# Two heads' keys from one matmul product, and a weight load split in two

## The chip, the cores and the metric

The kernel runs on one core of a Trainium2 chip. The metric is the device time of one execution in microseconds (us), the median of several runs. The engines are named as in the profile: PE is TensorE (PEld its weight loads), DVE is VectorE, ACT is ScalarE, POOL is GpSimd, and SP is SyncE, which here issues DMAs.

## What is computed

Two layers of a bidirectional encoder over 512 tokens of width 1024. Each layer projects x once and runs three kinds of attention side by side; then one output projection, a layer norm, a feed-forward part and another layer norm. The change is in the first kind, multi-head latent attention with six heads:

```python
ckv = rms_norm(h[..., o0:o0 + MLA_KV_RANK], mla_kv_norm[l])          # 128 wide
kva = (ckv @ mla_w_ukv[l]).reshape(B, S, MLA_HEADS, MLA_NOPE_DIM + MLA_V_DIM)
k_rope = jnp.broadcast_to(rope(k_rope, pos), (B, S, MLA_HEADS, MLA_ROPE_DIM))
ka = jnp.concatenate([kva[..., :MLA_NOPE_DIM], k_rope], axis=-1)     # 64 + 32
va = kva[..., MLA_NOPE_DIM:]                                         # 64
out_a = dense_attention(qa, ka, va, (MLA_NOPE_DIM + MLA_ROPE_DIM) ** -0.5)
```

The weight `mla_w_ukv` has 768 columns: for each of the six heads 64 columns that make its keys and then 64 that make its values.

## The kernel before, in words

All products are done in a split form: an operand is held as a high part `hi` and a low remainder `lo`, and `mm3` (line 160) makes a product of three matmuls, hi x hi, hi x lo and lo x hi, into one PSUM bank. So every tile that goes into a product is first copied by ScalarE (the high part) and then subtracted on VectorE or GpSimd (the low part).

`wload` (line 140) loads a weight: one DMA on SP's queue into a raw tile, a copy on ScalarE into `whi`, a subtraction into `wlo`.

The attention of all 16 heads is run by `attend` (line 322): units of one head and 128 queries each follow each other. A unit has three steps that run some units apart: `a` makes the scores (`sc`, line 251), the row minimum on VectorE (`nm`, line 261), the exponential on ScalarE (`pl`, line 263) and the scaling on GpSimd (line 266); `b` transposes the weights on TensorE (`ptr`, line 274) and splits them (`PTh` on ScalarE, `PTl` on VectorE, line 282); `c` multiplies them with the values (`po`, lines 292 and 293). Between the units fillers are run, generators that do the projections and prepare later heads; the table `W` says from which unit to which. The framework's scheduler then sets the instructions of each engine in an order of its own, so a change in one place can move rows elsewhere.

Latent heads come last, units 40 to 63. What prepares them are fillers:

- `latent_qv` (line 588) loads the query weights and `w_ukv` (line 591), makes the queries (`uq`), and then, for each of four token tiles, the values of all heads (`uv`, line 609) from the value columns, which it picks out of the 768 by stride; `mv` (lines 375, 376) are the split values.
- `mla_T(h)` (line 537), once for each head, in two steps: it transposes the head's queries (`tT` into `qkT`), and then makes the head's keys: three matmuls with the 64 key columns of this head, 512 tokens wide, into a bank of `ps_mm`; a DMA puts the shared rotary part `krT` below (line 544), and ScalarE and VectorE split the 64 rows (lines 546, 547) into the tile `kT`:

```python
wk = [w[:, 0, h * P:h * P + HD] for w in wkv[0]]
r = pqk.tile([P, 2, T], F32R, tag="q", name="kT")
mm3(pb[:HD], wk, (latT[2][:, 0], latT[2][:, 1]), True, True)
```

Two pools set limits here: `ps_mm` has two PSUM banks, which `uq`, `uv`, `tT`, `kT` and the output projection's first part (`opp`, line 633) share in turn; `pqk` has four buffers for `qkT` and `kT`, also in turn.

Of the kernel before, what the change touches and what calls it, by code (L numbers as in the profile page):

```python
# [10 lines left out]
F32 = mybir.dt.float32  # L11
F32R = mybir.dt.float32r
AF = mybir.ActivationFunctionType
ALU = mybir.AluOpType
AX = mybir.AxisListType

P = 128
T = 512
# [6 lines left out]
HD = 64  # L25
# [54 lines left out]
def encoder(ctx: ExitStack, tc, x, w_in, mla_q_norm, mla_kv_norm, w_uq, w_ukv, gqa_q_norm, gqa_k_norm, rel_bias,  # L80
            w_out, ln1_g, ln1_b, w_gate, w_up, w_down, ln2_g, ln2_b, tabs, onehot, neglnc, out):
    nc = tc.nc
    V, A, G, TE = nc.vector, nc.scalar, nc.gpsimd, nc.tensor
    LO = {k: V if c == 'v' else G for k, c in LOE.items()}
# [10 lines left out]
    pqk = pool("pqk", 4)  # L95
# [10 lines left out]
    ps_mm = pool("ps_mm", 2, space=PS)  # L106
# [4 lines left out]
    def bank(pl, name):  # L111
        return pl.tile([P, 512], F32, tag="b", name=name)
# [24 lines left out]
             "m": ((pmix, "m"), (pmix, "m"))}  # L137
    turn = {"raw": 0}

    def wload(src, shape, lo, ring="w", raw="w"):  # L140

        n = shape[1] * shape[2]
        if raw == "wd":
            turn["raw"] += 1
            raw = "wwdd"[turn["raw"] % 4]
        (hp, ht), (lp, lt) = parts[ring]
        r = raws[raw][0].tile([P, 1024], F32, tag=raws[raw][1], name="wraw")
        nc.sync.dma_start(r[:, :n].rearrange("p (a c) -> p a c", a=shape[1]), src)
        h = hp.tile([P, 1024], F32R, tag=ht, name="whi")
        A.copy(h[:, :n], r[:, :n])  # L150
        o = lp.tile([P, 1024], F32R, tag=lt, name="wlo")
        step = n // 2 if lo is G and SPLIT else n
        for c in range(0, n, step):
            lo.tensor_tensor(o[:, c:c + step], r[:, c:c + step], h[:, c:c + step].bitcast(F32), op=ALU.subtract)  # L154
        return (h[:, :n].rearrange("p (a c) -> p a c", a=shape[1]), o[:, :n].rearrange("p (a c) -> p a c", a=shape[1]))

    def krows(w, k0, nk, c0, c1):
        return w[k0 * P:(k0 + nk) * P, c0:c1].rearrange("(k p) c -> p k c", p=P)

    def mm3(ps, a, b, first, last, more=False):  # L160

        ah, al = a
        bh, bl = b
        TE.matmul(ps, ah, bh, start=first, stop=False, skip_group_check=more)  # L164
        TE.matmul(ps, ah, bl, start=False, stop=False, skip_group_check=more)  # L165
        TE.matmul(ps, al, bh, start=False, stop=last, skip_group_check=more)  # L166
# [238 lines left out]
    for l in range(DEPTH):  # L405
# [131 lines left out]
        def mla_T(h):  # L537
            assert ("q", h // 3) in told
            to_T(lambda t: tq[h // 3][:, t, h % 3, :], 96, mqk[h])
            yield  # L540
            pb = bank(ps_mm, "kT")
            wk = [w[:, 0, h * P:h * P + HD] for w in wkv[0]]
            r = pqk.tile([P, 2, T], F32R, tag="q", name="kT")
            nc.sync.dma_start(r[HD:96].bitcast(F32), krT[0][:32].bitcast(F32))
            mm3(pb[:HD], wk, (latT[2][:, 0], latT[2][:, 1]), True, True)
            A.copy(r[:HD, 0], pb[:HD])
            V.tensor_tensor(r[:HD, 1], pb[:HD], r[:HD, 0].bitcast(F32), op=ALU.subtract)
            mqk[h].append(r)
            yield

        def dil_qk(pair):
# [36 lines left out]
        def latent_qv():  # L588
            tq.extend(pxt.tile([P, NT, 3, 96], F32, tag="x", name="tq") for _ in range(2))
            wq = [wload(krows(w_uq[l], 0, 2, 288 * c, 288 * c + 288), (P, 2, 288), LO['uq']) for c in range(2)]  # L590
            wkv.append(wload(krows(w_ukv[l], 0, 1, 0, 768), (P, 1, 768), LO['kv']))
            yield
            for c in range(2):
                h, o = wq[c]
                for t in range(NT):
                    pb = bank(ps_mm, "uq")[:, :288]
                    ts = slice(t * P, (t + 1) * P)
                    for k in range(2):
                        mm3(pb, (latT[k][:, 0, ts], latT[k][:, 1, ts]), (h[:, k], o[:, k]), k == 0, k == 1)
                    A.copy(tq[c][:, t], pb.rearrange("p (h c) -> p h c", h=3))  # L600
                    yield
                tm = ppl.tile([P, T], F32, tag="l", name="qrt")[:, :384].rearrange("p (t h c) -> p t h c", t=NT, h=3)
                rope32(tq[c][:, :, :, 64:96], 3, tm)
                told.append(("q", c))
            h, o = (w[:, 0].rearrange("p (h c) -> p h c", h=6)[:, :, HD:] for w in wkv[0])
            for t in range(NT):
                pb = bank(ps_mm, "uv")[:, :6 * HD]
                ts = slice(t * P, (t + 1) * P)
                mm3(pb, (latT[2][:, 0, ts], latT[2][:, 1, ts]), (h, o), True, True)
                vt = pv_sb.tile([P, 6, 2, HD], F32R, tag="v", name="mv")  # L610
                split_v(vt, pb.rearrange("p (a c) -> p a c", a=6))
                mv_.append(vt)
                yield
# [53 lines left out]


        latT, krT, tq, mv_, wkv, dts, told = [], [], [], [], [], {}, []
        gqk, dqk, mqk = ([[] for _ in range(n)] for n in (2, 3, 6))  # L670
        heads = []
        for h in range(6):
# [33 lines left out]
        lqv, op = latent_qv(), out_part()  # L706
# [312 lines left out]
```

## Time and profile before

| | |
|---|---|
| median of 3 runs | 1259.31 us (1258.02 to 1260.97) |
| the profiled execution's own time | 1259.3 us |
| its span in the profile | 1257.5 us |
| TensorE busy | 1222.3 us, 97% |
| VectorE busy | 871.6 us, 69% |
| ScalarE busy | 661.9 us, 53% |
| GpSimd busy | 491.9 us, 39% |
| data moved by DMA | 153.26 MB, mean 122 GB/s |

The span is what the profile's rows cover; the execution's time has 1.8 us around it. Layer 1 begins in the trace at some 640 us; the latent heads are prepared and run at 130 to 260 us and again at 745 to 895 us. A share of busy time is a mean over stages; a row of the chain of waits says what was on the path that ended last in a stretch, and a row of the timeline when an instruction started and how long its engine had waited before it. A matmul's recorded length overlaps the next one's, so the time that one takes from TensorE is read from start to start, or from the chain.

### The profile page before, as it was taken

The page shows a single profiled execution, that of the slowest core. Times are in us where ns is not written, and L with a number is a line of the kernel's source. Part 1 is how long each engine was busy: PE and PEld are TensorE (multiplying, and loading weights), DVE is VectorE, ACT ScalarE, POOL GpSimd, SP SyncE. Part 2 cuts the span into 40 slices and gives each one's busy share as a digit, 9 for nine tenths or more (in the row PEclk, how much of TensorE's full clock was granted, in tenths as well). Part 3 has the DMA queues.
Part 4 walks back from the last instruction along what each step waited for, and adds up shares of the span by engine and source line. Part 5 has one row for each costly group of instructions (what it writes and reads, how often), then busy time and mean ns, then how long its engine had stood idle before and what let it go on. Part 6 is the DMA issues. An engine that isn't in the chain of part 4 may idle for free.

```text
span 1257.5 us, 20806 instructions
## 1 busy us (share of the span) xinstructions
PE 1222.3 (97%) x7816; PEld 1108.8 (88%) x7816; DVE 871.6 (69%) x1512; ACT 661.9 (53%) x1273; POOL 491.9 (39%) x508
## 2 busy tenths in 40 slices
PE   8999899999999999999999998999999999999996
PEld 7789788889999889998888897888899988999985
DVE  4369998597875447773664889966987743677546
ACT  4366786553654235652445667855355632466422
POOL 0345575568442024300345466645574400341004
PEclk9899999999999999999999999999999999999998
DMA  6623310326988348834535231105199953685343
GB/s 184 172 81 93 89 35 13 106 84 137 191 185 193 107 102 177 163 87 129 179 96 145 85 105 40 37 12 159 57 182 183 192 164 92 127 184 126 107 153 117
DMA packets 167692, 153.26 MB, mean 122 GB/s; under 512 B 9340, under 2 KB 136444, under 8 KB 167592
## 3 DMA queue, kind: packets, MB, share of 16 engines
q1 hardware_dynamic: 121228, 111.98, 30.4%
q0 software_dynamic: 46208, 39.86, 18.1%
q8 instruction: 62, 1.02, 0.3%
q14 instruction: 38, 0.31, 0.1%
q10 hardware_dynamic: 156, 0.09, 0.0%
HBM read 145.06 MB, written 2.12 MB: 117 GB/s over the span
## 4 chain that ended last, share of the span: by engine, by line
PE 82%; DVE 7%; POOL 3%; ACT 3%; DMA 2%; issue 2%; SPq 1%; DVEq 0%; ACTq 0%; POOLq 0%
PE u L164 10%; PE u L165 10%; PE u L166 10%; PE down L164 6%; PE down L166 6%; PE down L165 6%; PE sc L251 4%; PE ptr L274 3%; PE po L293 2%; PE po L292 2%; PE qkp L164 2%; PE qkp L166 2%; PE qkp L165 2%; PE tp L164 2%; PE tp L165 2%
## 5 line engine op out<-in xcount | busy, mean ns | idle before, releaser
L150 ACT CAST whi<-wraw 128x1024 fp32r<-128x1024 f32 (+4 forms) x132 | 127.3, 968 | 197.2 <-PE down L166 97.4
L154 DVE TENSOR_TENSOR wlo<-wraw,whi 128x1024 fp32r<-128x1024 f32 (+4 forms) x100 | 118.0, 1182 | 112.4 <-ACT whi L150 111.5
L266 POOL TENSOR_TENSOR pl<-pl,srec 128x512 f32<-128x512 f32 x128 | 136.2, 1066 | 145.6 <-DVE srec L265 132.2
L166 PE MATMUL u<-tf,wlo 128*128 128x256 f32 x608 | 170.6, 283 | 0.0
L165 PE MATMUL u<-tf,whi 128*128 128x256 f32 x608 | 170.6, 283 | 0.0
L164 PE MATMUL u<-tf,whi 128*128 128x256 f32 x608 | 167.1, 283 | 0.2 <-ACT u L919 0.2
L838 POOL DMA_DIRECT2D wsum<-in_ffn_w_up x76 | 72.4, 953 | 192.4 <-DVE wlo L895 192.0
L165 PE MATMUL down<-wlo,act 128*128 128x512 f32 x352 | 136.4, 389 | 0.0
L166 PE MATMUL down<-whi,act 128*128 128x512 f32 x352 | 136.1, 389 | 0.0
L164 PE MATMUL down<-whi,act 128*128 128x512 f32 x352 | 133.6, 390 | 0.0
L164 PE MATMUL u<-xF,whi 128*128 128x256 f32 x456 | 129.2, 283 | 0.6 <-ACT whi L889 0.6
L166 PE MATMUL u<-xF,wlo 128*128 128x256 f32 x456 | 129.0, 283 | 0.0
L165 PE MATMUL u<-xF,whi 128*128 128x256 f32 x456 | 129.0, 283 | 0.0
L165 PEld LDWEIGHTS u<-tf,whi 128*128 128x128 f32 x608 | 116.6, 192 | 0.4
L166 PEld LDWEIGHTS u<-tf,wlo 128*128 128x128 f32 x608 | 116.6, 192 | 0.0
L164 PEld LDWEIGHTS u<-tf,whi 128*128 128x128 f32 x608 | 114.3, 192 | 0.9 <-ACT u L919 0.4
L154 POOL TENSOR_TENSOR wlo<-wraw,whi 128x512 fp32r<-128x512 f32 (+2 forms) x64 | 76.8, 1222 | 79.8 <-ACT whi L150 76.5
L281 ACT CAST PTh<-ptr 128x512 fp32r<-128x512 f32 x128 | 74.8, 585 | 43.3 <-PE ptr L274 42.8
L894 ACT CAST whi<-wsum 128x512 fp32r<-128x512 f32 x76 | 47.1, 620 | 91.6 <-issue 52.2
L840 POOL DMA_DIRECT2D wsum<-in_ffn_w_up x38 | 57.1, 1630 | 92.7 <-DMA wsum<-in_ffn_w_up 92.7
L282 DVE TENSOR_TENSOR PTl<-ptr,PTh 128x512 fp32r<-128x512 f32 x128 | 87.3, 684 | 8.5 <-ACT PTh L281 7.2
L164 PEld LDWEIGHTS u<-xF,whi 128*128 128x128 f32 x456 | 87.5, 192 | 0.8 <-ACT whi L889 0.8
(220 smaller groups left out, 3452.9 us busy)
## 6 DMA issues: line engine op xcount, KB each, us to landing
wsum<-in_ffn_w_up POOLq DMA_DIRECT2D x114, 256.0 KB, 5.4
wraw<-in_ffn_w_down SPq DMA_DIRECT2D x50, 512.0 KB, 4.5
wraw<-in_ffn_w_gate SPq DMA_DIRECT2D x44, 512.0 KB, 4.9
wraw<-in_w_in SPq DMA_DIRECT2D x20, 512.0 KB, 4.6
wraw<-in_ffn_w_up SPq DMA_DIRECT2D x38, 256.0 KB, 3.0
wsum<-in_ffn_w_gate POOLq DMA_DIRECT2D x38, 256.0 KB, 7.4
wraw<-in_w_out SPq DMA_DIRECT2D x14, 512.0 KB, 3.8
dt<-tdr SPq DMA_DIRECT2D x12, 448.0 KB, 3.6
```

The lines of the kernel that those rows point to most:

```text
L150: A.copy(h[:, :n], r[:, :n])
L154: lo.tensor_tensor(o[:, c:c + step], r[:, c:c + step], h[:, c:c + step].bitcast(F32), op=ALU.subtract)
L164: TE.matmul(ps, ah, bh, start=first, stop=False, skip_group_check=more)
L165: TE.matmul(ps, ah, bl, start=False, stop=False, skip_group_check=more)
L166: TE.matmul(ps, al, bh, start=False, stop=last, skip_group_check=more)
L251: TE.matmul(sc, a, b, start=i == 0, stop=i == len(ops) - 1)
L266: G.tensor_tensor(pl, pl, r.to_broadcast([P, T]), op=ALU.mult)
L281: A.copy(ph[:, :, c:c + P], pb)
L282: V.tensor_tensor(plo[:, :, c:c + P], pb, ph[:, :, c:c + P].bitcast(F32), op=ALU.subtract)
L838: G.dma_start(v, rows(*first_))
L840: G.dma_start(v, rows(*then), accum_op=ALU.add)
L894: A.copy(h[:, c], src[i])
```

## The change

`mla_T` makes the keys of two heads at once, at each even head: three matmuls with 128 columns instead of twice three with 64. The 128 rows of the bank are split in two halves of 64 rows, each into its own `kT` tile with its own DMA of `krT`; the odd head's tile is kept in `mlk` until its turn. So that the key columns of neighbouring heads are neighbours, the load of `w_ukv` is split: `wload` gets a parameter `by`, and two DMAs bring first all 384 key columns and then all 384 value columns, in pieces of 64 columns. The values are then one run of columns instead of a strided pick.

```diff
-            pb = bank(ps_mm, "kT")
-            wk = [w[:, 0, h * P:h * P + HD] for w in wkv[0]]
-            r = pqk.tile([P, 2, T], F32R, tag="q", name="kT")
-            nc.sync.dma_start(r[HD:96].bitcast(F32), krT[0][:32].bitcast(F32))
-            mm3(pb[:HD], wk, (latT[2][:, 0], latT[2][:, 1]), True, True)
-            A.copy(r[:HD, 0], pb[:HD])
-            V.tensor_tensor(r[:HD, 1], pb[:HD], r[:HD, 0].bitcast(F32), op=ALU.subtract)
-            mqk[h].append(r)
+            if h % 2 == 0:
+                kT = bank(ps_mm, "kT")
+                wk = [w[:, 0, h * HD:(h + 2) * HD] for w in wkv[0]]
+                mm3(kT, wk, (latT[2][:, 0], latT[2][:, 1]), True, True)
+                for e in range(2):
+                    pb = kT[64 * e:64 * e + 64]
+                    r = pqk.tile([P, 2, T], F32R, tag="q", name="kT")
+                    nc.sync.dma_start(r[HD:96].bitcast(F32), krT[0][:32].bitcast(F32))
+                    A.copy(r[:HD, 0], pb)
+                    V.tensor_tensor(r[:HD, 1], pb, r[:HD, 0].bitcast(F32), op=ALU.subtract)
+                    mlk[h + e] = r
+            mqk[h].append(mlk[h])
...
-            wkv.append(wload(krows(w_ukv[l], 0, 1, 0, 768), (P, 1, 768), LO['kv']))
+            wkv.append(wload([w_ukv[l].rearrange("p (h s c) -> p s h c", h=6, s=2)[:, i] for i in range(2)], (P, 2, 384), LO['kv'], by=2))
...
-            h, o = (w[:, 0].rearrange("p (h c) -> p h c", h=6)[:, :, HD:] for w in wkv[0])
+            h, o = (w[:, 1] for w in wkv[0])
...
-        nc.sync.dma_start(r[:, :n].rearrange("p (a c) -> p a c", a=shape[1]), src)
+        if by == 1:
+            nc.sync.dma_start(r[:, :n].rearrange("p (a c) -> p a c", a=shape[1]), src)
+        else:
+            for i in range(by):
+                nc.sync.dma_start(r[:, i * n // by:(i + 1) * n // by].rearrange("p (a c) -> p a c", c=src[i].shape[-1]), src[i])
```

The scheduler sets the order anew from here on. Three places of it follow, of the first layer; line numbers of the new kernel are 5 to 10 higher. TensorE has 7816 matmuls before and 7798 now.

TensorE, where the first latent head's scores begin, before (the key product of head 0 stands 16 rows ahead; `kT_2036` is its split tile, the bank is `kT_2035`, and `uv_2079` is the third of the four value products):

```order
L251 MATMUL sc_2159<-kT_2036,qkT_2002 128x512
L274 MATMUL ptr_2171<-tab_114,pl_2046 128x128 x4
L164 MATMUL uv_2079<-whi_1623,lat_1786 128x384
L165 MATMUL uv_2079<-wlo_1625,lat_1786 128x384
L166 MATMUL uv_2079<-whi_1623,lat_1786 128x384
L251 MATMUL sc_2159<-kT_2036,qkT_2002 128x512 x2
L164 MATMUL uv_2104<-whi_1623,lat_1786 128x384
L165 MATMUL uv_2104<-wlo_1625,lat_1786 128x384
```

And now (the bank of both heads' keys is `kT_2036`, the split tiles are `kT_2040` and `kT_2044`, the third value product is `uv_2084`):

```order
L256 MATMUL sc_2156<-kT_2040,qkT_2003 128x512
L279 MATMUL ptr_2168<-tab_114,pl_2051 128x128 x4
L256 MATMUL sc_2156<-kT_2040,qkT_2003 128x512 x2
L169 MATMUL uv_2084<-whi_1624,lat_1787 128x384
L170 MATMUL uv_2084<-wlo_1626,lat_1787 128x384
L171 MATMUL uv_2084<-whi_1624,lat_1787 128x384
L297 MATMUL po_2196<-PTh_2140,gv_801 128x256
L279 MATMUL ptr_2187<-tab_114,pl_2094 128x128 x4
```

The third value product has moved behind the other two matmuls of the first score product, and the fourth further back.

VectorE in the same place, before:

```order
L547 TENSOR_TENSOR kT_2036<-kT_2035,kT_2036 64x512
L376 TENSOR_TENSOR mv_2076<-uv_2072,mv_2076 128x6x64
L265 RECIPROCAL srec_2094<-ssum_2092 128x1
L261 TENSOR_REDUCE nm_2123<-sc_2119 128x1
L282 TENSOR_TENSOR PTl_2136<-ptr_2130,PTh_2135 128x4x128
L282 TENSOR_TENSOR PTl_2136<-ptr_2171,PTh_2135 128x4x128
L376 TENSOR_TENSOR mv_2083<-uv_2079,mv_2083 128x6x64
```

And now:

```order
L556 TENSOR_TENSOR kT_2040<-kT_2036,kT_2040 64x512
L381 TENSOR_TENSOR mv_2081<-uv_2077,mv_2081 128x6x64
L270 RECIPROCAL srec_2099<-ssum_2097 128x1
L266 TENSOR_REDUCE nm_2128<-sc_2124 128x1
L287 TENSOR_TENSOR PTl_2141<-ptr_2135,PTh_2140 128x4x128
L556 TENSOR_TENSOR kT_2044<-kT_2036,kT_2044 64x512
L287 TENSOR_TENSOR PTl_2141<-ptr_2168,PTh_2140 128x4x128
```

The odd head's key subtraction, which stood 13 rows further back, now stands five instructions behind the even head's.

SP's queue at the load of `w_ukv`, before and now:

```order
L646 DMA dt<-tdr 128x896
L148 DMA wraw<-in_mla_w_ukv 128x768
L148 DMA wraw<-in_ffn_w_up 128x8x128
L148 DMA wraw<-in_w_out 128x2x512
L148 DMA wraw<-in_w_out 128x512
```

```order
L656 DMA dt<-tdr 128x896
L153 DMA wraw<-in_mla_w_ukv 128x6x64 x2
L149 DMA wraw<-in_ffn_w_up 128x8x128
L149 DMA wraw<-in_w_out 128x2x512
L149 DMA wraw<-in_w_out 128x512
```

One transfer has become two in the same place; the loads behind it stand as before.

## Rows read from the trace of the kernel before

**Rows 1.** The page, part 1: busy us (share of span), instructions.
```profile
PE 1222.3 (97%) x7816; PEld 1108.8 (88%) x7816; DVE 871.6 (69%) x1512; ACT 661.9 (53%) x1273; POOL 491.9 (39%) x508
```

**Rows 2.** Chain of waits, 170 to 203 us: start us, us, engine, tile, line.
```profile
188.67 0.24 PE kT L164
188.91 0.23 PE kT L165
189.14 0.24 PE kT L166
...
201.77 0.23 PE opp L165
```

**Rows 3.** The same chain, ten us earlier.
```profile
182.47 0.61 DVE kT L547
...
183.12 0.44 PE uv L164
...
183.93 0.46 PE sc L251 x2
```

**Rows 4.** Timeline of VectorE: start us, us, instruction.
```profile
182.39 0.68 DVE L547 TENSOR_TENSOR kT<-kT 64x512 fp32r<-64x512 f32 x1
182.99 0.54 DVE L376 TENSOR_TENSOR mv<-uv,mv 128x384 fp32r<-128x384 f32 x1
...
183.53 0.66 DVE L261 TENSOR_REDUCE nm<-sc 128x1 f32<-128x512 f32 x1
184.12 1.27 DVE L282 TENSOR_TENSOR PTl<-ptr,PTh 128x512 fp32r<-128x512 f32 x2
185.31 0.54 DVE L376 TENSOR_TENSOR mv<-uv,mv 128x384 fp32r<-128x384 f32 x1
```

**Rows 5.** Chain of waits in the second layer, 785 to 845 us.
```profile
798.85 0.61 DVE kT L547
799.50 0.44 PE uv L164
```

**Rows 6.** Chain of waits, 125 to 215 us.
```profile
130.29 3.29 DMA wraw<-in_mla_w_ukv
133.66 0.83 ACT whi L150
...
143.54 0.39 PE po L293
```

**Rows 7.** Chain of waits in the second layer, 738 to 770 us.
```profile
745.89 3.37 DMA wraw<-in_mla_w_ukv
...
759.22 0.58 PE po L293
```

**Rows 8.** DMA issues: tiles, queue, count, KB each, median us from issue to landing.
```profile
kT<-krT SPq DMA_DIRECT2D x12, 128.0 KB, 2.3
...
wraw<-in_mla_w_ukv SPq DMA_DIRECT2D x2, 384.0 KB, 3.3
...
gg<-in_gqa_q_norm SPq DMA_DIRECT2D x2, 128.0 KB, 10.4
```

**Rows 9.** SP's DMA queue, 16 to 22 us, then 128 to 142: packets, MB, share.
```profile
DMA packets 1355, 0.43 MB, mean 71 GB/s; under 512 B 987, under 2 KB 1355, under 8 KB 1355
...
q1 hardware_dynamic: 1355, 0.43, 28.5%
...
q1 hardware_dynamic: 1600, 1.70, 40.7%
```

**Rows 10.** Timeline of TensorE: the wait before an instruction, in brackets, and its releaser.
```profile
33.16 0.77 PE L164 MATMUL qkp<-xTh,whi 128*128 128x512 f32 x1 [2.09 <-DVE nl L389]
...
143.54 0.39 PE L293 MATMUL po<-PTl,dv 128*128 128x256 f32 x1 [2.31 <-DVE PTl L282]
...
904.48 0.63 PE L187 MATMUL xtr<-tab,xtok 128*128 128x128 f32 x4 [1.50 <-DVE mv L210]
```

**Rows 11.** Busy us by engine in two stretches, then granted clock, DMA share, GB/s.
```profile
143.00:146.00 3.00, 2.46 (x15) 2.46 (x16) 3.00 (x8) 1.09 (x3) 0.71 (x1) 0.79 0.46 164
146.00:149.00 3.00, 3.00 (x15) 2.61 (x15) 2.91 (x8) 1.47 (x4) 1.04 (x1) 0.64 0.30 86
```

More of the change, by code (lines that the diff above doesn't have):

```diff
@@ L138, in encoder, with wload @@
     turn = {"raw": 0}
-    def wload(src, shape, lo, ring="w", raw="w"):
+    def wload(src, shape, lo, ring="w", raw="w", by=1):
         n = shape[1] * shape[2]
@@ L669, in encoder @@
         latT, krT, tq, mv_, wkv, dts, told = [], [], [], [], [], {}, []
+        mlk = {}
         gqk, dqk, mqk = ([[] for _ in range(n)] for n in (2, 3, 6))
```

## The prediction

> **What bounds the kernel now.** Read the page first: TensorE is busy for 1222.3 of 1257.5 us [rows 1]. So a microsecond of work taken from TensorE is worth a microsecond only where TensorE does not go on to wait for somebody, and the question is which wait ends last in the two places that the change touches. The chain of waits answers that. In the stretch where the key products stand, it runs through TensorE: the three matmuls of a key product follow each other on it, 0.24, 0.23 and 0.24 us [rows 2]. Just ahead of that the chain runs through VectorE: it ends its work on a key tile at 183.08 and the third value product starts at 183.12 [rows 3]. The second layer repeats this [rows 5]. And some fifty us earlier the chain runs through the very load that the change splits: its transfer, then ScalarE's copy of it, and from there over ScalarE and VectorE to a TensorE that has waited 2.31 us [rows 6, 10]; the same in the second layer [rows 7]. All three places are on the path, so all three parts of the change count.
>
> **Products: less work.** A head's key product is three matmuls of 64 columns over 512 tokens and takes 0.24 + 0.23 + 0.24 = 0.71 us, say 0.70 [rows 2]. A matmul with a 128-column weight over 512 tokens, as in the output projection, takes 0.23 too [rows 2], so the paired product costs what one head's costs, and three of six products fall away in each layer: 3 x 0.70 = 2.1 us of TensorE, 4.2 in both. The copies and subtractions stay: two of 64 rows for each pair, as before.
>
> **Products: a bank held longer.** One PSUM bank now holds two heads' keys, and it is free only after the second subtraction on VectorE. The pool has two banks. In the order before, the third value product (uv) needs the bank that the first subtraction frees at 183.08 [rows 3]. In the new order VectorE does five instructions between that and the second subtraction's end: the value subtraction with the reciprocal behind it (182.99 to 183.53, 0.54), the minimum (183.53 to 184.12, 0.59), one subtraction of transposed weights (two take 184.12 to 185.31, so 0.60) and the second key subtraction itself (182.39 to 182.99, 0.60) [rows 4]. Sum 2.33 us: the value product starts at 183.12 + 2.33 = 185.45. Ahead of it TensorE can do the two score products that used to stand behind it, 0.46 us [rows 3]; they need the first key subtraction, so they run from 183.12 to 183.58. Then TensorE stands still for 1.87 us, where it had none of this wait. Everything behind on TensorE is queued behind it: score products, transposes, and so the whole softmax chain. VectorE does the same work as before, one subtraction earlier, so it does not catch up for anybody. Price 1.87 us a layer, 3.7 in both. Bounds: 0, if VectorE's order already bounds the next ten us so that TensorE's wait is only one that it would have had later; and 1.87 + 0.6 if one more subtraction of that size [rows 4] slips in front of what TensorE wants next.
>
> The later pairs hold their bank too, and longer: the odd head's tile takes the buffer of the odd head before, so its copy waits for that head's last score product. What covers this, in the new order, is a score product of three matmuls, 0.7 us at 0.23 each [rows 2], and a dozen smaller matmuls on TensorE between that last score product and the next output product that wants the bank, against one copy and one subtraction of about 0.6 [rows 4] each. I price it at nothing; without that cover it would be up to 1.2 us a pair.
>
> **The load.** Before, one transfer of 384 KB in rows of 3 KB: 3.29 and 3.37 us to the landing [rows 6, 7]. Now two transfers, each of 128 x 6 = 768 pieces of 256 bytes, 1536 in all. Nothing in the trace is quite like it. In a stretch where most packets were under 512 bytes, 1355 packets took 28.5% of 16 engines for 6 us: 27.4 us / 1355 = 20 ns each. In the stretch of this load, 1.70 MB took 40.7% of 16 engines for 14 us: 54 ns a KB [rows 9]. By these the load takes 384 x 54 ns / 16 = 1.3 us of the engines now, and 1536 x 20 ns / 16 = 1.9 us then: 0.6 us more. Low end 0: the bytes are the same and one more issue is added, so no gain. High end 1.5: 128 KB land in 2.3 us and 384 KB in 3.3 [rows 8], so 256 KB cost 1.0 and 384 KB 1.5, and at double the time for each byte that is added once more. The slowest row with 256-byte pieces, 10.4 us for 128 KB [rows 8], I set aside as an end: those were issued at the start behind all of the input. I take 0.6, from the row whose packets are nearest in size. ScalarE waits for this load in its own order, VectorE's subtraction behind it waits for ScalarE, and the softmax of the running head is queued behind both; the chain has no slack [rows 6], so it counts in full: 1.2 in both layers. The loads behind it on SP's queue move by one issue and are wanted tens of us later; they cost nothing.
>
> **Sum.** -4.2 + 3.7 + 1.2 = +0.7 us, on the profiled execution's 1259.3, which is also the median of the runs (1259.31). **Forecast 1260.0: no change.** A measurement of this kernel can tell about 0.2%, 2.5 us, from no change.
>
> A part that I can't price: the scheduler has also set the rest of the program in another order, up to the feed-forward part, where TensorE has almost no idle time. I allow 1 us to both sides.
>
> **Rivals.**
> *The bank wait costs nothing* (faster). VectorE has no gap from 182 to 185 [rows 4]; if it bounds this stretch, TensorE would have waited for it soon anyway and its stall is absorbed. For it: TensorE's wait and VectorE's work overlap there. Against: after 183.12 the chain stays with TensorE [rows 2, 3]. Then -4.2 + 1.2 = -3.0: 1256.3. Chance 0.23.
>
> *The stall lowers TensorE's clock* (slower). After the wait of 2.31 us the granted clock was 0.79 and then 0.64 over two stretches of 3 us [rows 10, 11], that is, part of the time at 1.2 instead of 2.4 GHz: 3 x 0.21 + 3 x 0.36 = 1.7 us lost. The new stall of 1.87 lies between waits of 2.09 and 2.31, and one of 1.50 [rows 10]. The place is the third value product; it decides from whether the stall is more like the 2.31 or the 1.50. If it falls in both layers, 3.4 more: 1263.4. In one layer only it is 1261.7, still inside what can't be told apart. Chance of both 0.17.
>
> *The small pieces land late* (slower). At double the time for each byte the load costs 1.5 instead of 0.6 in each layer, and two issues with their own completion can add to it: 1260.0 + 1.8 = 1261.8, or some more. For it: this load is on the chain in both layers [rows 6, 7]. Against: the 20 ns for a small packet [rows 9]. The Trainium skill, in DMA: Bandwidth & Descriptors, section Specifications, names 512 bytes as the least transfer for the full rate and says that below it the engine reads, modifies and writes. By that rule the high end of the load's price would be the right one; no run here shows it yet. Chance 0.15.
>
> *The change doesn't do what it says* is out: the order shows 18 matmuls fewer and the new products with 128 columns.
>
> **How the numbers follow.** Forecast 0.45, at 1260.0. Faster by over 0.2% (under 1256.8): the first rival, and a little of the forecast's own spread, 0.25. Slower by over 0.2% (over 1261.8): the second rival, most of the third, 0.29 with the spread. The same: 0.46. The range runs from the first rival's 1256.3 to the clock's 1263.4, each with half of the 1 us allowed for the new order beyond it, and leaves out about 2 in 10: 1255.8 to 1263.9.
>
> **What would show it.** In the profile after: 18 key matmuls fewer, each of the remaining with 128 columns and 0.23 us apart; a wait of TensorE of 1.6 to 2.0 us before the third value product in each layer, released by the second key subtraction on VectorE, and no clock under 1.00 behind it; the two halves of the load landing 3.7 to 4.2 us after the first issue, and TensorE's wait that was 2.31 us about 0.6 longer. Wrong would be: no wait before that value product (then the first rival), a clock of 0.8 or less between it and the next ten us (the second), or a landing after 5 us (the third). If all these come out as said and the time is still off by over 2 us, the cause lies in the order of the rest.

## The result, and the profile after

The changed kernel takes 1266.45 us (median of 6 runs, 1263.74 to 1268.28) against 1259.12 (6 runs): ratio 1.0061, 95% interval 1.0048 to 1.0073. It is **slower by 7.3 us**; forecast was 1260.0, no change, with 1263.9 as the upper end. The execution profiled below took 1268.15 us, one of the longer ones.

The page answers to [rows 1]: 18 matmuls fewer, and TensorE is busy for longer.

```profile
PE 1225.0 (97%) x7798; PEld 1109.2 (88%) x7798; DVE 878.7 (69%) x1512; ACT 663.4 (52%) x1273; POOL 494.3 (39%) x508
```

**The load.** The chain of waits of the changed kernel at the split load, for [rows 6] (start us, us, what):

```profile
131.58 4.59 DMA wraw<-in_mla_w_ukv
...
136.28 0.84 ACT whi L155
...
146.13 0.58 PE po L298
```

The first issue starts at 130.48, almost where it was, the second half lands at 136.17, 5.7 us later, where 3.3 had been. ScalarE's copy begins 2.6 us later than before, and so does everything behind it up to the output product. The wait right ahead of that product is 2.11 us and not longer than the 2.31 of before [rows 10]: TensorE loses the time sooner. In the second layer ([rows 7] before) the landing takes 4.26 us from the first issue, where it took 3.37:

```profile
752.33 3.60 DMA wraw<-in_mla_w_ukv
756.03 0.83 ACT whi L155
```

TensorE's clock stands in the windows of the same stretch, with the columns of [rows 11] (the column before the last two is the granted clock):

```profile
137.00:140.00 3.00, 1.30 (x10) 0.82 (x9) 2.17 (x5) 3.00 (x11) 1.58 (x2) 1.00 0.44 136
140.00:143.00 3.00, 2.15 (x10) 1.38 (x10) 3.00 (x7) 2.16 (x5) 2.92 (x5) 0.80 0.08 29
143.00:146.00 3.00, 0.92 (x2) 0.29 (x1) 2.96 (x8) 2.53 (x8) 2.69 (x4) 0.50 0.16 38
146.00:149.00 3.00, 2.87 (x13) 2.87 (x14) 2.10 (x7) 1.40 (x3) 0.36 (x1) 0.50 0.40 137
149.00:152.00 3.00, 3.00 (x14) 2.70 (x13) 2.92 (x8) 0.58 (x1) 1.04 (x1) 0.50 0.12 34
152.00:155.00 3.00, 2.74 (x22) 2.43 (x21) 2.82 (x6) 2.92 (x8) 1.04 (x1) 0.99 0.49 146
```

TensorE was busy for 4.4 of the 9 us from 137 to 146, and it ran at 1.2 GHz from about 142 to 152, where before only a part of 143 to 149 was at that level [rows 11].

**The keys.** TensorE's timeline in the second layer (wait and releaser in brackets):

```profile
800.39 0.48 PE L169 MATMUL kT<-lat,whi 128*128 128x512 f32 x1
...
803.69 0.39 PE L298 MATMUL po<-PTl,gv 128*128 128x256 f32 x1 [0.78 <-DVE PTl L287]
...
806.14 0.34 PE L169 MATMUL uv<-whi,lat 128*128 128x384 f32 x1
...
807.38 0.63 PE L279 MATMUL ptr<-tab,pl 128*128 128x128 f32 x4 [0.20 <-DVE PTl L287]
...
808.55 0.34 PE L169 MATMUL uv<-whi,lat 128*128 128x384 f32 x1
...
812.76 0.66 PE L279 MATMUL ptr<-tab,pl 128*128 128x128 f32 x4 [0.33 <-POOL pl L271]
...
818.87 0.96 PE L256 MATMUL sc<-kT,qkT 96*128 96x512 f32 x3 [0.29 <-ACT pl L268]
```

The forecast wait of 1.87 us before the third value product (uv at 806.14) isn't there. There are instead four of 0.2 to 0.8 us, spread over 15 us and released by three engines. The longest of them stands in the kernel before too, in the same place:

```profile
797.63 0.38 PE L293 MATMUL po<-PTl,gv 128*128 128x256 f32 x1 [0.78 <-DVE PTl L282]
```

So 0.8 us of waiting is new. VectorE's timeline shows what happens at the bank:

```profile
804.85 0.67 DVE L556 TENSOR_TENSOR kT<-kT 64x512 fp32r<-64x512 f32 x1
805.45 0.54 DVE L381 TENSOR_TENSOR mv<-uv,mv 128x384 fp32r<-128x384 f32 x1
...
806.57 0.67 DVE L287 TENSOR_TENSOR PTl<-ptr,PTh 128x512 fp32r<-128x512 f32 x1
807.27 0.69 DVE L556 TENSOR_TENSOR kT<-kT 64x512 fp32r<-64x512 f32 x1
807.99 0.69 DVE L287 TENSOR_TENSOR PTl<-ptr,PTh 128x512 fp32r<-128x512 f32 x1
```

The third value product cannot be writing the keys' bank: it starts at 806.14, and VectorE reads that bank for the odd head from 807.27 to 807.96. Only the fourth (808.55) comes behind that, and no wait is recorded ahead of it.

The same rows show something else. The even head's subtraction (804.85) is followed by the next instruction after 0.60 us, 0.07 before its own end: VectorE's instructions overlap a little. The odd head's, which reads rows 64 to 127 of the bank and writes rows 0 to 63, begins 0.03 us after the one ahead of it has ended, and the next begins 0.72 us later, 0.03 after its end. So it takes 0.22 us more of VectorE's time than the same subtraction unpaired. All 24 odd subtractions in the four profiles that pair the products and subtract each half by itself (after, the pairing alone, both copies first, and the pairing held in the old order) stand apart like this. None of those of the odd head moved up do, and none of the 128-row subtractions of the first run with a DMA.

On ScalarE the copy of the pair's second half waits, and not for the product:

```profile
801.38 0.60 ACT L555 CAST kT<-kT 64x512 fp32r<-64x512 f32 x1
...
805.55 0.58 ACT L555 CAST kT<-kT 64x512 fp32r<-64x512 f32 x1 [1.16 <-DVE kT L556]
```

The windows from the first key product to the first output product of the shared part (us; then busy us of TensorE, its weight loads, VectorE, ScalarE, GpSimd), first of before:

```profile
794.36:817.64 23.28, 22.40 (x145) 18.94 (x144) 22.55 (x45) 19.50 (x45) 14.64 (x14) 1.00 0.11 29
```

and of after:

```profile
800.39:824.46 24.07, 22.27 (x139) 18.35 (x138) 23.08 (x45) 19.90 (x44) 14.67 (x15) 1.00 0.11 28
```

VectorE is busy for 22.55 of 23.28 us in this stretch before, with 45 instructions, and TensorE for 22.40. TensorE has six matmuls fewer in it after, and the stretch is 0.79 us longer.

**Where the time went.** The table takes the start of certain instructions on TensorE's timeline and gives, for each kernel's one profiled execution, how much longer each stretch is than before (first layer / second layer, us). "Keys" runs from the first key product to the first product of the shared output part (opp); "attention and handover" from there to the last gate product of the first block of the feed-forward part (the handover is its end, where the output projection gives way to the feed-forward part); "then" from there to the first down product. Before they take 23.32 / 23.28, 112.60 / 113.47 and 80.18 / 79.74 us.

| kernel | keys | attention and handover | then |
|---|---|---|---|
| after | +0.72 / +0.79 | +0.67 / +1.08 | +0.14 / +0.58 |
| split load alone | +0.03 / +0.01 | -0.13 / +0.01 | -0.12 / 0.00 |
| pairing alone | +0.71 / +0.80 | +0.68 / +2.38 | +0.13 / +0.57 |
| both copies first | +0.72 / +0.76 | +0.99 / +2.67 | +0.13 / +0.57 |
| odd head moved up | -0.01 / +0.05 | +0.35 / +0.41 | +0.14 / +0.57 |
| the same, short products | -0.19 / -0.15 | +0.50 / +0.50 | +0.13 / +0.56 |
| one term of three | +0.54 / +0.60 | +2.85 / +0.99 | -0.86 / +0.57 |
| one due time moved | -0.02 / +0.04 | +3.62 / +0.62 | +0.12 / +0.57 |

For after these add to 4.0 us, of the 8.8 by which its profiled span is longer. Of the rest, 3.7 us lie ahead of the first layer's first key product and 0.8 between the first layer's first down product and the second layer's first key product, the two parts that hold the load. These single profiles are rough there: kernels with the same order up to the first key product and the same load reach it up to 3.6 us apart (176.67 to 180.24). The delay of the copy is steadier. From the first issue of the load to ScalarE's copy it takes 3.37 and 3.45 us before (first and second layer), 5.80 and 4.36 after, 4.84 and 4.91 with the split load alone, and 3.3 to 3.6 in every profile with one plain load.

### The profile page after: what moved, and what is told of

Read it like the earlier page. It is cut to its first block, busy times and chain, and to the rows that moved or that the text cites. A ratio compares the mean times of both kernels' runs of the same rounds, so it can differ in the third digit from the quotient of the medians.

```text
span 1266.3 us, 20769 instructions
## 1 busy us (share of the span) xinstructions
PE 1225.0 (97%) x7798; PEld 1109.2 (88%) x7798; DVE 878.7 (69%) x1512; ACT 663.4 (52%) x1273; POOL 494.3 (39%) x508
## 4 chain that ended last, share of the span: by engine, by line
PE 81%; DVE 7%; ACT 3%; POOL 3%; DMA 2%; issue 2%; DVEq 0%; SPq 0%; ACTq 0%; POOLq 0%
PE u L169 10%; PE u L170 10%; PE u L171 10%; PE down L169 6%; PE down L171 6%; PE down L170 6%; PE sc L256 4%; PE ptr L279 3%; PE tp L169 2%; PE tp L170 2%; PE tp L171 2%; PE qkp L169 2%; PE qkp L170 2%; PE qkp L171 2%; PE po L298 2%
```

## The experiments

Each ratio is against runs of the kernel before on the same chip in the same session; 0.1% is 1.26 us. Two things can be compared without talk of order, since a reordering scheduler stands between code and program: the run with the split load alone and the one with two plain loads have the order of the kernel before on every engine, and after has the order of the pairing alone, but for the load's issue and VectorE's two halves of the weight's subtraction.

**The load alone** (each head keeps its own product):

```diff
-    wk = [w[:, 0, h * HD:(h + 2) * HD] for w in wkv[0]]
+    wk = [w[:, 0, h * HD:(h + 1) * HD] for w in wkv[0]]
```

> The load is split as in the change, but each head still has its own key product of 64 columns. Theory A (the second issue of the split load comes late, ScalarE's copy of the weight waits for it, and the chain and TensorE's clock in the first layer pay for it): nearly the whole loss is here, 1263 to 1268 us, with the copy's wait at about 3 us in the first layer and 1.6 in the second, as in the change (3.09, 1.65; before 0.66). Theory B (the pairing with its held bank costs more than it saves, the load little): 1259.5 to 1261, by the 0.6 us a layer that I forecast. Theory C (any change of order in this stretch costs some us in the handover to the feed-forward part): about 1262, and the excess appears behind the attention.

Measured 1.0029 (1.0018 to 1.0041), 1263.99 us. Half of the loss, with no change of order at all. Its copy waits 2.14 us (timelines of ScalarE and SP, first layer):

```profile
135.16 0.83 ACT L155 CAST whi<-wraw 128x768 fp32r<-128x768 f32 x1 [2.14 <-DMA wraw<-in_mla_w_ukv]
130.32 1.66 SPq L153 DMA_DIRECT2D wraw<-in_mla_w_ukv  x2
```

**The pairing alone** (one plain load; the copy and the subtraction of the weight put the columns side by side):

```diff
-    wkv.append(wload([...], (P, 2, 384), LO['kv'], by=2))
+    wkv.append(wload(krows(w_ukv[l], 0, 1, 0, 768), (P, 1, 768), LO['kv'], perm=6))
+    # in wload: A.copy and lo.tensor_tensor read r as "p (h s c) -> p s h c"
```

> The key products are paired as in the change, but the weight is loaded by one DMA as before, and ScalarE's copy and the subtraction behind it put the key columns side by side. Theory A: the load's cost goes and the products' gain (4.2 us by the duration of 0.23) stays in part: 1255 to 1259.5 us, the copy's wait back at 0.7 us in the first layer, the granted clock at 2.4 GHz until about 144.5 us. Theory B: 1263 to 1267, with TensorE late by as much between the first key product and the first output product as in the change. Theory C: about 1262.

Measured 1.0030 (1.0018 to 1.0042), 1263.58 us. The other half. Neither theory A nor B holds alone: each part costs nearly 3.8 us, and they add up. The reordering copy takes 0.84 us, where the plain one took 0.83, VectorE's two halves of the weight's subtraction 0.07 more than the whole, and the wait for the load is back where it was (0.66 before):

```profile
134.34 0.84 ACT L155 CAST whi<-wraw 128x768 fp32r<-128x768 f32 x1 [0.75 <-DMA wraw<-in_mla_w_ukv]
130.89 0.35 SPq L148 DMA_DIRECT2D wraw<-in_mla_w_ukv  x1
```

**Two plain loads** (the kernel before, two issues, long pieces):

```diff
+    for i in range(2):
+        nc.sync.dma_start(r[:, i * 384:(i + 1) * 384], w_ukv[l][:, 384 * i:384 * i + 384])
```

> The kernel before, with its load of the weight cut into two DMAs of 384 adjacent columns each (pieces of 1536 bytes); nothing else changes. If the second issue is what costs (theory A as I read the trace: 0.6 us an issue, 1.05 us apart): the copy's wait is near 2 to 3 us in the first layer, 1262 to 1267 us. If the small pieces of 256 bytes are what costs: the copy's wait grows by at most the 0.35 us of an issue, 1259 to 1260.5.

Measured 1.0004 (0.9994 to 1.0014), 1261.10 us: no difference that can be told.

```profile
132.54 0.83 ACT L155 CAST whi<-wraw 128x768 fp32r<-128x768 f32 x1 [1.14 <-DMA wraw<-in_mla_w_ukv]
128.69 1.13 SPq L153 DMA_DIRECT2D wraw<-in_mla_w_ukv  x2
```

Against the split load alone only the size of the pieces differs, 1536 or 256 bytes, and by the two ratios that is 3.2 us of the 3.7. Both issues together end 1.13 us after the start, or 1.66. From issue to landing one half of 192 KB takes 2.7 us here (DMA issues; last number median us to landing)

```profile
wraw<-in_mla_w_ukv SPq DMA_DIRECT2D x2, 192.0 KB, 2.7
```

and 3.3 with the small pieces, 4.0 in the profile of after. The DMA engines' share of the stretch from 128 to 142 us hardly differs (44.4% with long pieces, 41.4% with small ones), so the price isn't the engine time that I had worked it out from; it lies in issue and landing. The Trainium skill, in DMA: Bandwidth & Descriptors, section Specifications, names 512 bytes as the least transfer for the full rate. That the smaller pieces cost agrees with these runs; a lower rate of the engines is not what their share shows.

**The second half issued by ScalarE:**

```diff
-    nc.sync.dma_start(
+    (A if i else nc.sync).dma_start(
```

> As the run with the split load alone, but the second DMA is issued by ScalarE. If the time between the two issues on one queue is what costs: the second half leaves as early as the first, and most of the loss goes, 1259 to 1262 us, less what an issue takes of ScalarE. If the pieces of 256 bytes land late however they are issued: 1263 to 1268, as the split load alone.

Measured 1.0017 (1.0007 to 1.0026), 1262.81 us. Between the two: the copy starts 4.45 and 4.21 us after the first issue, where it was 4.84 and 4.91 with both on SP. Its own wait falls further in the first layer, from 2.14 to 1.11, but part of that is only that in this run the copy of another weight has moved ahead of it; and the issue holds ScalarE's queue for 0.56 to 0.63 us.

**Pairing, both copies first** (so that the second copy doesn't wait for the first subtraction):

```diff
     for e in range(2):
         A.copy(r[:HD, 0], kT[64 * e:64 * e + 64])
-        V.tensor_tensor(...)
+    for e, r in enumerate(rs):
+        V.tensor_tensor(...)
```

> As the pairing alone (plain load), but both of ScalarE's copies of a pair's bank are written ahead of both of VectorE's subtractions. Serial theory (in the changed kernel the second copy waits 1.2 us for the first subtraction, which stands behind 4 us of VectorE's queue, so the second subtraction and the bank's release come late): the wait on that subtraction goes, the second one follows the first at once, and of the 3.6 us that the pairing alone lost 1 to 3 us come back, 1260.5 to 1262.5. Early theory (the odd head's copy and subtraction, done a head too early in a stretch that VectorE bounds, are the loss): no gain, 1262.5 to 1264.5. Bound theory (the saved products were never on the path there): 1260 or more in both cases, not below the kernel before.

Measured 1.0036 (1.0023 to 1.0050), 1264.27 us. A miss for the serial theory. The wait of the copy is gone, and the last matmul of the value products starts 6.9 us after the first key product in both layers (before 6.6; pairing alone 8.5). The bank is free early, and the time doesn't move, though the order behind it is another one too. The stretch of the keys is as long as with the pairing alone. So no sign is left that the held bank costs.

**The odd head moved up** (two products of 64 columns in two banks, nothing paired):

```diff
+    for e in range(2 if h % 2 == 0 else 0):
+        wk = [w[:, 0, (h + e) * P:(h + e) * P + HD] for w in wkv[0]]
```

> The kernel before, with the odd head's key product, its copy and its subtraction moved up behind those of the even head; two products of 64 columns in two banks, nothing paired. Early theory: the loss of the pairing shows without any pairing, and on top the 4.2 us of products are not saved: 1263 to 1268. Serial theory: each bank is released by its own subtraction, so little is lost: 1259.5 to 1261.5.

Measured 1.0014 (1.0005 to 1.0023), 1260.93 us. In the handover TensorE's order is that of after, row by row, and the table shows the loss there. It also shows that the stretch of the keys keeps its length in this run, where nothing is paired.

**Pairing with a DMA for the odd half** (one copy and one subtraction of 128 partitions for both heads):

```diff
+    A.copy(r[:, 0], kT)
+    V.tensor_tensor(r[:, 1], kT, r[:, 0].bitcast(F32), op=ALU.subtract)
+    nc.sync.dma_start(o[:HD].bitcast(F32), r[HD:].bitcast(F32))
```

> As the pairing alone (plain load), but the bank is taken out by one copy and one subtraction of 128 partitions, and a DMA moves the odd head's half to its own tile, whose latency of 2 to 4 us lies ahead of the first use. If VectorE and ScalarE bound the stretch from the first key product to the first output product: 3 subtractions of 0.69 us and 3 copies of 0.58 us fewer a layer, and the bank is free early: 1254 to 1258.5 us. If the order a head early is what costs: 1261 to 1264. If the DMAs in a chain land late: TensorE waits at the first score of heads 0, 2 or 4 behind a landing, 1260 to 1265.

Measured 1.0066 (1.0054 to 1.0079), 1267.31 us. The third case came: TensorE waits for the key tile's chain of transfers.

```profile
191.10 1.66 PE L259 MATMUL sc<-kT,qkT 96*128 96x512 f32 x6 [1.84 <-DMA kT<-krT]
```

**One term of three** (the kernel before with 24 of its 36 key matmuls left out):

```diff
-    mm3(pb[:HD], wk, (latT[2][:, 0], latT[2][:, 1]), True, True)
+    TE.matmul(pb[:HD], wk[0], latT[2][:, 0], start=True, stop=True)
```

> The kernel before, with one of the three matmuls of each key product: 24 of 36 matmuls of 0.23 us are left out, and with them the small parts of weight and latent in the keys. If these matmuls are on the path that sets the end (as I priced them): 5.5 us less, 1253.5 to 1255. If VectorE bounds the stretches that they lie in: 1257 to 1260, with TensorE's waits between the first key product and the first output product grown by about what is left out.

Measured 1.0045 (1.0032 to 1.0057), 1264.38 us. By the price of my first step this should give back 5.5 us; it takes 4.8 more (medians of its session). In the stretch of the keys eight matmuls are gone, and it is 0.60 us longer. But the new order has also put one more group of transposes into it, four on TensorE and their subtraction of 0.6 us on VectorE (141 matmuls and 46 instructions of VectorE below, not 137 and 45). For the same work the stretch is about as long as before, and not 1.8 us shorter:

```profile
798.16:822.04 23.88, 22.16 (x141) 18.28 (x140) 23.15 (x46) 19.82 (x45) 14.65 (x15) 1.00 0.11 28
```

The loss itself lies behind that, in an order that differs in every engine. In the first layer TensorE reaches the gate products before ScalarE and VectorE have their input, and its clock falls (timeline, then a window with clock 0.58):

```profile
279.31 0.39 PE L164 MATMUL gate<-xF,whi 128*128 128x256 f32 x1 [1.25 <-ACT xF L190]
283.39 0.58 PE L165 MATMUL gate<-xF,whi 128*128 128x256 f32 x1 [3.34 <-DVE xF L191]
...
280.00:285.00 5.00, 1.66 (x8) 1.61 (x8) 4.96 (x9) 0.81 (x1) 1.55 (x2) 0.58 0.58 164
```

**The odd head moved up, with short products:**

```diff
+    c = 32 if e else T    # columns of the second and third matmul
```

> As the run with the odd head's product moved up behind the even one (two banks, nothing paired), but two of the three matmuls of the odd head take 32 columns in place of 512: 12 matmuls of 0.23 us shrink to almost nothing, with the small parts of most odd keys left out; TensorE's order in the handover to the feed-forward part is that of the run it is compared with, row by row. If TensorE's time is what counts in this stretch (my first step): 2.5 us below that run's ratio of 1.0014, so about 0.9994, 1258 to 1259.5 us. If VectorE bounds it: within 0.8 us of that run, 1260.5 to 1262.

Measured 1.0005 (0.9993 to 1.0018), 1260.26 us. Between the two expectations, and the intervals of the two runs overlap: 2.3 us less of TensorE (start to start, both layers) bought 0.7 us by the medians or 1.1 by the ratios, if anything. The stretch of the keys tells more, since every engine has there the order of the run it is compared with (windows of the second layer, first with full and then with short products):

```profile
794.02:817.35 23.33, 22.52 (x146) 18.96 (x144) 22.54 (x45) 19.46 (x44) 14.67 (x15) 1.00 0.11 29
794.13:817.26 23.13, 22.05 (x145) 18.72 (x144) 22.42 (x45) 19.43 (x44) 14.67 (x15) 1.00 0.12 29
```

The key products take 2.27 us of TensorE in it instead of 3.03, and the stretch is 0.19 us shorter: a quarter comes back. TensorE's wait for VectorE ahead of the output product grows from 0.62 to 0.90.

**No subtraction of the keys on VectorE** (zeros from GpSimd for the small part), first without and then with the pairing:

```diff
-    V.tensor_tensor(r[:HD, 1], pb[:HD], r[:HD, 0].bitcast(F32), op=ALU.subtract)
+    G.memset(r[:HD, 1].bitcast(F32), 0.0)
```

> The kernel before, with VectorE's subtraction of each key taken away and the small part of the keys filled with zeros by GpSimd: 12 times 0.67 us less on VectorE, TensorE's work the same, and the same order in the handover. If VectorE bounds the stretch from the first key product to the first output product, where 4 of the 6 subtractions of a layer lie: 1.5 to 2.5 us less a layer, 1254 to 1257 us. If TensorE bounds it (my first step): no gain, 1258.5 to 1260.

> The pairing alone (plain load), with VectorE's subtraction of the keys replaced in the same way, so that the bank is free after ScalarE's copies. If VectorE's queue is what took the pairing's gain: this is below the pairing alone (ratio 1.0030) by 4 us or more, 1256 to 1260 us. If the order of the handover takes the gain: it stays 1 to 3 us above the run that leaves out the subtraction without pairing, since TensorE's order in the handover is that of the changed kernel.

Measured 1.0023 (1.0013 to 1.0032) and 1.0029 (1.0018 to 1.0039). Inconclusive as a test of VectorE, because an instruction of the rotary part on VectorE became much longer in both runs (`tq`; the first row is of before, the others of the run without the pairing):

```profile
178.65 1.28 DVE L585 TENSOR_TENSOR tq<-tq,tab 128x384 f32<-128x384 f32 x1
...
177.83 3.31 DVE L585 TENSOR_TENSOR tq<-tq,tab 128x384 f32<-128x384 f32 x1
...
181.67 0.54 DVE L586 TENSOR_TENSOR tq<-tq,qrt 128x384 f32<-128x384 f32 x1
```

For 3.28 us, from 177.45 to 180.73, GpSimd runs three instructions back to back, and the `tq` of 3.31 us ends 0.4 us after the last of them; the next `tq` has GpSimd idle beside it and takes 0.54. The transposed weights behind it came late, so that the stretch of the keys grew by 2.56 and 1.76 us without the pairing; with it, it grew by 0.32 and 0.37. What the missing subtractions are worth can't be read from these two runs.

**One due time moved** (the kernel before, same instructions):

```diff
-         ... op=(51, 65), ...
+         ... op=(51, 66), ...
```

> The kernel before with one number of its table of due times moved by one (the last output products due at step 66 in place of 65): the same instructions, of which some 200 of TensorE's 7051 rows stand elsewhere, most of them in the handover to the feed-forward part. It measures what an order by itself is worth there. If the order counts as I think from the run with the odd head moved up (0.9 and 0.3 us lost between the first output product of the own block and the last gate product): a change of 1 us or more in one direction, 1260.5 to 1263, or 1256 to 1258.5. If the order is worth nothing: 1259 to 1260.

Measured 1.0031 (1.0018 to 1.0043), 1264.29 us. This change of order by itself costs as much as the whole pairing. In the new order there is a place in the handover that makes TensorE wait for ScalarE, and the clock is 0.52 behind it:

```profile
263.29 0.45 PE L292 MATMUL po<-PTh,mv 128*128 128x256 f32 x1 [2.46 <-ACT PTh L281]
...
264.00:267.00 3.00, 3.00 (x8) 2.32 (x9) 2.06 (x4) 0.00 (x0) 0.83 (x1) 0.52 0.25 73
```

**Orders held by edges.** In the last three runs edges between instructions fix TensorE's order: the pairing alone with the handover of before; before with the handover of after; the pairing by DMA with the order of before throughout.

```diff
+    for a, b in zip(names, names[1:]):
+        tc.add_manual_dep(log[b], a, edge, reason="order")
```

> The pairing alone (plain load), with edges that hold TensorE from the first output product of the own block to the first sums of the feed-forward part in exactly the order of the kernel before; the attention stays as the pairing makes it. If the order of the handover is what costs (order theory): the 1.0 and 0.7 us lost there come back, ratio 1.0010 to 1.0018, 1261 to 1262.5. If what is lost lies in the attention or in the pairing itself: 1.0025 to 1.0035, 1263 to 1264.5.

> The kernel before, with TensorE held in the handover to the changed kernel's order, and nothing else touched (TensorE's order in the attention is that of before, row by row). Order theory: slower by the 1.0 and 0.4 to 0.7 us that the changed kernel loses there, ratio 1.0010 to 1.0020, 1261.2 to 1262.5. If the order costs nothing by itself: 0.9995 to 1.0007.

> The pairing with one copy and one subtraction for both heads and a DMA for the odd head's half (ratio 1.0066 in its own order), with edges that hold TensorE in the order of the kernel before from the first key product on, less the 9 products a layer that are gone. Order theory: most of the loss goes, and the saved work counts: 1256 to 1261 us. If the saved products were never on the path, or the DMAs in a chain land late: 1262 to 1268, with TensorE's waits behind the landing of the key tiles.

Measured 1.0029 (1.0018 to 1.0040), 1.0008 (1.0000 to 1.0017) and 1.0339 (1.0325 to 1.0352). The handover's order costs the kernel before about 1 us (0 to 2 by the interval), and giving the pairing the old order brings nothing: so TensorE's order in the handover is about a quarter of the loss in one kernel, and undoing it alone doesn't help the other, where the other engines still have the pairing's order. In the third run TensorE waits 30.3 us in 6 places for key tiles to land; a fixed order has no way around a late transfer.

```profile
PE sc L95 <- DMA kT<-krT: 30.3, 6, 6.1
```

## Why the prediction was wrong

**Step "Products: less work" failed, in what it is worth.** Its size was right: nine matmuls a layer are gone, and the start-to-start time of the key products falls from 4.5 to 2.3 us a layer. But I counted it in full because the chain ran through TensorE, and did not read the same stretch for VectorE, whose timeline I had without a gap [rows 4]. The chain itself runs over VectorE alone for the 5.5 us ahead of the third value product (first and last row of it):

```profile
177.58 0.69 DVE PTl L282
...
182.47 0.61 DVE kT L547
```

Four of the six products of a layer stand where VectorE is busy for 22.55 of 23.28 us. Where key matmuls were shortened in an unchanged order, a quarter of their time came back. With one term of three the stretch got no shorter for the same work. That most of the saved time does not come back is shown; that VectorE's queue sets the length of this stretch is argued from its busy time and from TensorE's longer wait for it, since the run that was to show it was spoilt by the long `tq`.

The same step says that the copies and subtractions stay as before. Their number does, but each odd head's subtraction takes 0.22 us more of VectorE, 0.44 in the stretch of the keys. That is over half of the 0.72 to 0.80 us that this stretch grows by in the paired kernels; that it is a cause of the growth is argued from where it stands, as no run removes it alone.

**Step "a bank held longer" failed in its mechanism.** No stall of 1.87 us appeared. I had carried the bank of the third value product over from the old order; in the new one it does not take the keys' bank, and with that bank freed early the time stayed. The rival "the bank wait costs nothing" was right on the bank and wrong on its time, since it kept the 4.2 us of products. The loss of 0.72 and 0.79 us in the stretch of the keys belongs to the pairing: the run that moves the odd head up without pairing doesn't have it, every paired run that subtracts each half by itself has it.

**Step "the load" was mis-sized.** Forecast 1.2 us in both layers, measured 3.7 alone and 3.9 on top of the pairing (difference of the ratios). I took the price from the DMA engines' time for a packet [rows 9]; the time went into two longer issues and a later landing. The third rival had the mechanism, and its sign, a landing after 5 us, came in the first layer (5.7). Its high end of 1.5 a layer is just what the copy is late by with the split load alone, 1.47 and 1.46 us. Where the other 0.8 of the 3.7 goes stays open. A later copy can also leave TensorE idle for longer and at the lower clock: the mean granted clock over the runs is 0.9896 with the split load alone (9 runs) against 0.9915 before (33 runs). But the runs of both that have the same clock, 0.992, are still 3.1 us apart (1262.87, 3 runs, against 1259.73, 6 runs), so most of the price is not clock.

**The clock rival** fell for its place: no clock under 1.00 in the stretch of the keys, and the pairing alone has the mean clock of before over its runs (0.9911, 0.9915).

**The order of the rest**, allowed for with 1 us to both sides, was too little. One due time alone moved the kernel by 3.9 us. Of the pairing's 3.8 us, 1.5 to 1.8 come with moving the odd head up as well (table row and ratio of that run), 1.5 lie in the stretch of the keys, and the rest, somewhat under 1, is spread over attention and handover. Which instruction's place costs that last part stays open.

In sum: forecast -4.2 + 3.7 + 1.2; measured about +3.8 for products, bank and order together, and +3.7 to +3.9 for the load. The 3.7 us for a stall that never came stood against the 4.2 us that did not come back, so the forecast was closer than its steps. No version tried here beats the kernel before; the nearest are the two plain loads and the short products (which leave out most of the small parts of the odd keys), both within what can't be told from no change.

## What to carry to other kernels

Before work is taken off an engine, look whether another one fills the same stretch: a busy share of 97% of TensorE over the whole program says nothing about the 23 us in which VectorE is 97% busy as well. Cut a load into small pieces only where nobody waits for it, and let the copy that reads it anyway do the sorting: here that cost 0.01 us on ScalarE and 0.07 on VectorE. When two results share a bank, look at the rows that each half is read from and written to: here the half that changes rows took 0.22 us more of VectorE. And where a scheduler sets the order, a change is always two changes; the three runs here that do the same work in another order lost 1.0, 1.8 and 3.9 us, so compare against the same order, or against a null change such as one due time moved.

## What was not expected of the hardware

The same short waits cost the clock in one execution and not in another. At the start of the second layer TensorE waits 0.78 and 0.68 us before, and 0.75 and 0.68 in the pairing alone; behind them the clock is 1.00 (windows of before)

```profile
642.60:645.60 3.00, 2.89 (x17) 2.57 (x18) 2.80 (x5) 1.40 (x3) 0.84 (x1) 1.00 0.00 0
645.60:648.60 3.00, 3.00 (x20) 2.96 (x19) 0.92 (x2) 0.59 (x1) 0.00 (x0) 1.00 0.02 5
```

and 0.70, then 0.73, in the other:

```profile
645.00:648.00 3.00, 2.72 (x11) 2.40 (x12) 2.65 (x5) 1.58 (x4) 1.01 (x1) 0.70 0.00 0
648.00:651.00 3.00, 3.00 (x16) 2.97 (x15) 0.40 (x1) 0.00 (x0) 0.00 (x0) 0.73 0.02 5
```

It is worth about 1.5 us in that stretch. Of 17 profiles 5 have it: 4 of the 7 with a pairing, 1 of the 10 without, and after has not. Over all runs the pairing alone shows no lower clock than before, so I don't count it to the change. It is part of why single executions of one kernel lie up to 7.4 us apart (one due time moved), and why a profile's stretches need the runs beside them: the +2.38 of the pairing alone and the +2.67 of both copies first in the table have such a stretch at 1.2 GHz in them, at 887 to 892 us, worth 1.3 us in the first by the difference from after.
